# The up product of a feed-forward block, from feature-major to token-major in eleven tiles

## The chip, the cores and the metric

The kernel runs on one core of one Trainium2 chip. The metric is the device time of one execution in microseconds, as the median of several runs. Everything is float32 outside; inside, each operand of a large product is split into two fp32r parts (hi and lo), and a product is three matmuls: hi x hi, lo x hi, hi x lo.

## The reference

One layer of an encoder for 256 tokens of width 2048: two attention mixers on one normalised input, merged by gates, an output projection, and a feed-forward block with norms before and behind it. The change concerns the feed-forward block and the seam ahead of it:

```python
mixed = (g_sb * y_sb + g_mla * y_mla) @ w_out[l]
h = h + rms_norm(mixed, norm_post_mix[l])

gu = rms_norm(h, norm_pre_ffn[l]) @ w_gate_up[l]     # 2048 x 11264
g, up = gu[..., :D_FF], gu[..., D_FF:]               # D_FF = 5632
h = h + rms_norm((jax.nn.silu(g) * up) @ w_down[l], norm_post_ffn[l])
```

`rms_norm(x, gain)` is x / sqrt(mean(x^2) + 1e-6) * gain.

## The kernel before

Weights come from HBM in units of 128 x 1024 float32 (512 KB), each a DMA on SyncE's queue into one of four `raw` buffers. `unit` (line 87) splits a unit: ScalarE copies it to fp32r (`hi`, line 100), VectorE subtracts (`lo`, line 101); there are four buffers of each. TensorE then streams.

There are two forms of product. `pair` (line 155) is feature-major: a 128 x 128 block of weights is the stationary operand, and the activations stream past it, once 512 columns wide (hi and lo parts of 256 tokens, line 171) against the hi weights and once 256 wide (hi part alone, line 173) against the lo weights. Its result has features on the partitions and tokens on the columns, and hi and lo sums lie side by side, so that `fold` (line 179) has to add them. `token` (line 185) is token-major: 128 tokens are the stationary operand, 512 columns of weights stream past, three times (lines 207 to 209). The up product (`gu`) is in 44 `pair`s of 128 gate and 128 up features, 16 k-tiles each; the output projection (`wout`) and the down product (`wd`) are in `token` form, four blocks of 512 columns each.

Accumulators are pairs of PSUM banks (`mm_pair`), two pairs in all. Four more banks (`at_bank`) serve transposes and small products. 52 slots of 2 KB per partition (`slot`) hold what lives longer.

The seam. The last block of `wout` ends its first 128 tokens four units ahead of the second 128. As a half ends, `after_mix` sums its squares (ScalarE, line 658), takes the root (`neg_rsqrt`), scales and adds (`residual`, VectorE, line 701). The sums go through a multiplication with `norm_pre_ffn` (`gffn`, GpSimd, line 703; for the first quarter of the second half, in `first_parts`, as a scale on the copy instead), then through TensorE transposes (`turned`, line 710, or `first_residual`, line 723) into `hs`, the feature-major input of `gu`, again as hi and lo (lines 713 and 714, 730 and 732). The factor `r2` of the second norm comes later: it is worked out while the first `pair`s run, spread over the partitions by two small matmuls (line 761), and multiplied in `fold`. `hidden` then applies SiLU, multiplies gate and up, and splits the result, quarter tile by quarter tile of the hidden features, into `hid`, which is the stationary operand of `wd` as it stands.

The order on each engine is set by a scheduler from the order in which the code is written and its own estimates; `at_unit(n, f)` hangs a piece of work behind the n-th unit, and `tc.issue_after` keeps a group from being put ahead of a given instruction.

Of the kernel before, what the change touches and what calls it, by code (L numbers as in the profile page):

```python
# [52 lines left out]
def block_kernel(ctx: ExitStack, tc: tile.TileContext, a: dict, out: bass.AP):  # L53
# [101 lines left out]
    def pair(name, stream, K, per, rhs, first=None, eng=None, middle=None, after=None):  # L155
        ps = mm_pair(f"{name}_ps")
        for u in range(K // per):
            cuts = (4 if u == 0 else 2) if first else 1
            with ExitStack() as order:
                if after and u >= after[0]:  # L160
                    for ins in after[1:]:
                        order.enter_context(tc.issue_after(ins))
                hi, lo = unit(stream, per * 2 * P, cuts, eng(u) if eng else None, first and (lambda c: first(u, c)))
# [451 lines left out]

    gffn = []
    for n in range(4):
        g_t = slot(f"gffn{n}")
        G.dma_start(g_t.rearrange("p a b -> p (a b)"),
# [280 lines left out]
```

## Time and profile before

| | us |
|---|---|
| median of 3 runs (1410.33, 1410.45, 1412.1) | 1410.45 |
| profiled execution, first to last instruction | 1409.0 |
| TensorE busy in it | 1383.6 |
| up product, first to last matmul start | 660.7 to 1160.0 |
| down product | 1160.1 to 1399.5 |

The profile is of one execution. Times in its rows are microseconds from the span's start. A matmul's duration overlaps with the next one's, so what a step costs is the distance from one start to the next. The profile's "idle before" of an engine tells what it waited for; only waits on the chain that ends last cost time. The granted clock of TensorE has two levels, 1.0 (2.4 GHz) and 0.5 (1.2 GHz), and a mean over a stretch lies in between.

### The profile page before, as it was taken

To read this page: it belongs to the slowest core of one execution; us is meant where nothing else is said; L and a number is where in the kernel's file an instruction comes from. 1 tells how busy PE (TensorE), PEld (TensorE's weight loads), DVE (VectorE), ACT (ScalarE), POOL (GpSimd) and SP (SyncE) were. 2 spreads that over 40 slices of the span, in tenths; PEclk is the share of its full clock that TensorE was granted. 3 is DMA by queue.
4 is the path that set the end of the run, shared out by engine and by line. 5 is a ranking of instruction groups with operands and counts; after the bars stand their busy time and mean duration, and the time that the engine had idled before them with its cause. 6 is when DMAs were issued, how large, how long until landed. Compare 5 with 4: busy or idle time off the path is not lost.

```text
span 1409.0 us, 19102 instructions
## 1 busy us (share of the span) xinstructions
PE 1383.6 (98%) x7372; PEld 1186.8 (84%) x7372; DVE 883.6 (63%) x1109; ACT 710.7 (50%) x959; POOL 71.6 (5%) x93
## 2 busy tenths in 40 slices
PE   7999999999999999997999999999999999999997
PEld 6888888888888888886888888888888888888886
DVE  7996965555555687548666666666656565444444
ACT  7554454466658555445544444444444454434343
POOL 3210000000002200003000000000000001000000
PEclk9999999999999999999999999999999999999999
DMA  7565655455556765653655565556555556666653
GB/s 240 183 209 164 195 164 161 154 171 173 165 181 234 244 193 186 194 190 105 207 182 188 185 188 186 186 187 185 189 182 192 182 191 222 191 195 192 192 193 117
DMA packets 74668, 262.00 MB, mean 186 GB/s; under 512 B 8528, under 2 KB 9680, under 8 KB 74448
## 3 DMA queue, kind: packets, MB, share of 16 engines
q1 hardware_dynamic: 72720, 254.87, 56.7%
q0 software_dynamic: 1424, 5.24, 1.1%
q8 instruction: 58, 0.95, 0.3%
q10 hardware_dynamic: 432, 0.66, 0.1%
q14 instruction: 34, 0.28, 0.1%
HBM read 258.64 MB, written 2.10 MB: 185 GB/s over the span
## 4 chain that ended last, share of the span: by engine, by line
PE 93%; DVE 4%; ACT 1%; issue 1%; DMA 0%; SPq 0%; POOL 0%; DVEq 0%; ACTq 0%
PE gu_ps L171 23%; PE gu_ps L173 12%; PE gate_ps L171 8%; PE wd_ps L207 6%; PE wd_ps L208 6%; PE wd_ps L209 6%; PE gate_ps L173 4%; PE wo_ps L637 4%; PE q_sb_ps L171 2%; PE k_sb_ps L171 2%; PE wo_ps L638 2%; PE wout_ps L207 2%; PE wout_ps L208 2%; PE wout_ps L209 2%; PE q_sb_ps L173 1%; PE k_sb_ps L173 1%
## 5 line engine op out<-in xcount | busy, mean ns | idle before, releaser
L171 PE MATMUL gu_ps<-hs,hi_w_gu 128*128 128x512 f32 x1408 | 498.1, 399 | 0.2 <-DVE hs L732 0.2
L173 PE MATMUL gu_ps<-hs,lo_w_gu 128*128 128x256 f32 x1408 | 396.0, 281 | 0.0
L171 PEld LDWEIGHTS gu_ps<-hs,hi_w_gu 128*128 128x128 f32 x1408 | 264.8, 188 | 65.6 <-DVE hs L732 0.5
L101 DVE TENSOR_TENSOR lo_w_gu<-raw_w_gu,hi_w_gu 128x1024 fp32r<-128x1024 f32 x175 | 216.0, 1235 | 159.8 <-ACT hi_w_gu L100 159.7
L100 ACT ACTIVATE hi_w_gu<-raw_w_gu 128x1024 fp32r<-128x1024 f32 x176 | 185.7, 1056 | 195.0 <-issue 116.9
L173 PEld LDWEIGHTS gu_ps<-hs,lo_w_gu 128*128 128x128 f32 x1408 | 266.6, 189 | 0.1
L101 DVE TENSOR_TENSOR lo_w_down<-raw_w_down,hi_w_down 128x1024 fp32r<-128x1024 f32 x88 | 110.9, 1262 | 119.1 <-ACT hi_w_down L100 118.9
L171 PE MATMUL gate_ps<-xs,hi_w_gate 128*128 128x512 f32 x512 | 180.7, 398 | 0.0
L100 ACT ACTIVATE hi_w_down<-raw_w_down 128x1024 fp32r<-128x1024 f32 x88 | 93.3, 1061 | 135.5 <-PE wd_ps L208 125.1
L173 PE MATMUL gate_ps<-xs,lo_w_gate 128*128 128x256 f32 x512 | 143.2, 280 | 0.0
L207 PE MATMUL wd_ps<-hi_w_down,hid 128*128 128x512 f32 x352 | 137.2, 390 | 0.0
L208 PE MATMUL wd_ps<-hi_w_down,hid 128*128 128x512 f32 x352 | 137.1, 390 | 0.0
L209 PE MATMUL wd_ps<-lo_w_down,hid 128*128 128x512 f32 x352 | 137.1, 389 | 0.0
L101 DVE TENSOR_TENSOR lo_w_gate<-raw_w_gate,hi_w_gate 128x1024 fp32r<-128x1024 f32 x64 | 78.4, 1230 | 68.5 <-ACT hi_w_gate L100 68.5
L171 PEld LDWEIGHTS gate_ps<-xs,hi_w_gate 128*128 128x128 f32 x512 | 96.3, 188 | 22.5
L100 ACT ACTIVATE hi_w_gate<-raw_w_gate 128x1024 fp32r<-128x1024 f32 x64 | 67.5, 1056 | 58.2 <-PE gate_ps L171 46.5
L173 PEld LDWEIGHTS gate_ps<-xs,lo_w_gate 128*128 128x128 f32 x512 | 96.6, 189 | 0.0
L207 PEld LDWEIGHTS wd_ps<-hi_w_down,hid 128*128 128x128 f32 x352 | 66.1, 188 | 14.1 <-DVE r L665 0.3
L209 PEld LDWEIGHTS wd_ps<-lo_w_down,hid 128*128 128x128 f32 x352 | 66.1, 188 | 13.7
L208 PEld LDWEIGHTS wd_ps<-hi_w_down,hid 128*128 128x128 f32 x352 | 66.1, 188 | 13.5
L101 DVE TENSOR_TENSOR lo_w_out<-raw_w_out,hi_w_out 128x1024 fp32r<-128x1024 f32 x32 | 39.2, 1225 | 37.0 <-ACT hi_w_out L100 36.8
L100 ACT ACTIVATE hi_w_out<-raw_w_out 128x1024 fp32r<-128x1024 f32 x32 | 33.9, 1061 | 43.9 <-PE wout_ps L208 34.7
(346 smaller groups left out, 2197.5 us busy)
## 6 DMA issues: line engine op xcount, KB each, us to landing
raw_w_gu<-in_w_gu SPq DMA_DIRECT2D x176, 512.0 KB, 3.5
raw_w_down<-in_w_down SPq DMA_DIRECT2D x88, 512.0 KB, 4.3
raw_w_gate<-in_w_gate SPq DMA_DIRECT2D x64, 512.0 KB, 3.6
raw_w_o<-in_w_o SPq DMA_DIRECT2D x32, 512.0 KB, 3.6
raw_w_out<-in_w_out SPq DMA_DIRECT2D x32, 512.0 KB, 3.5
raw_w_lat<-in_w_lat SPq DMA_DIRECT2D x16, 512.0 KB, 4.7
raw_w_q<-in_w_q SPq DMA_DIRECT2D x16, 512.0 KB, 4.1
raw_w_k<-in_w_k SPq DMA_DIRECT2D x16, 512.0 KB, 3.5
```

The costliest lines, as they stand in the source:

```text
L100: split_ins[0] = S.activation(hi[:, cs], raw[:, cs], AF.Copy)
L101: mi = (eng or V).tensor_tensor(lo[:, cs], raw[:, cs], hi[:, cs].bitcast(F32), op=ALU.subtract)
L171: TE.matmul(ps[:, j, :], lhsT=hi[:, o:o + P], rhs=r, start=k == 0, stop=False, skip_group_check=True)
L173: mm = TE.matmul(ps[:, j, 0:T], lhsT=lo[:, o:o + P], rhs=r[:, 0], start=False, stop=k == K - 1, skip_group_check=True)
L207: TE.matmul(ps[t], lhsT=l[:, 0, ts], rhs=hi[:, cs], start=k == 0, stop=False)
L208: TE.matmul(ps[t], lhsT=l[:, 1, ts], rhs=hi[:, cs], start=False, stop=False)
L209: mm = TE.matmul(ps[t], lhsT=l[:, 0, ts], rhs=lo[:, cs], start=False, stop=k == K - 1)
L637: TE.matmul(ps[:, j, :], lhsT=hi[:, o:o + P], rhs=r, start=k == 0, stop=False, skip_group_check=True)
L638: mm = TE.matmul(ps[:, j, 0:T], lhsT=lo[:, o:o + P], rhs=r[:, 0], start=False, stop=k == 7, skip_group_check=True)
```

## The change

The up product becomes token-major. It is done in 11 tiles (`up`) of 512 gate and 512 up columns; a unit is one k-tile of both (`up_unit`). For each k-tile and each half of the tokens there are six matmuls of 512 columns: three into the gate bank and three into the up bank. Each half has a pair of banks, so a tile holds all four. Within a tile the halves are offset: the first half does `head` k-tiles alone at the start (six in the first tile, two in the others), and ends two k-tiles ahead of the second. `up_out` takes a half out of its banks: SiLU with the factor r2 as a scale per partition on ScalarE, and one VectorE product. The result has tokens on the partitions, so `up_turn` transposes it on TensorE, four 128 x 128 blocks to a group, two groups a tile, hung behind units of the next tile, and splits it into hi and lo for `wd`.

`norm_pre_ffn` moves into the weight split: `up_unit` scales with the gain of the k-tile's rows, on ScalarE in the copy and on VectorE as a three-operand instruction. The four loads of `gffn` and GpSimd's eight products go, as do `fold`, `hidden` and the small matmuls of `r2` for this product. The four k-tiles that come first are split in halves into slots, not buffers. Both halves of the tokens now go through `residual` and `turned` alike, and `first_residual`, `first_parts` and `later_residual` go; the first transposes are hung one unit earlier (6 for `TURN` = 7). The weights are laid out accordingly; their bytes and their units are the same.

```diff
-def pair(name, stream, K, per, rhs, first=None, eng=None, middle=None, after=None):
+def pair(name, stream, K, per, rhs, first=None):
...
-        r1s[t] = neg_rsqrt(ss1, t, "r1", None if t else lambda: mg_part(ps, t, 3))
-        if t == 0:
+        r1s[t] = neg_rsqrt(ss1, t, "r1", lambda: mg_part(ps, t, 3))
+        with tc.issue_after(ready[0][1]):
             for n in range(4):
-                residual(0, n)
-        else:
-            tp = first_residual()
-            with tc.issue_after(ready[0][1]):
-                first_parts(tp)
-                mg_part(ps, 1, 3)
-                for n in range(1, 4):
-                    turned(0, n)
+                residual(t, n)
...
         V.scalar_tensor_tensor(x_t, mg[t, n], r1s[t], x_t, op0=ALU.mult, op1=ALU.add)
-        hg = tmp.tile([P, 512], F32, tag="t2", name="hg", bufs=6)
-        G.tensor_tensor(hg, x_t, flat(gffn[n]), op=ALU.mult)
-        hgs[t, n] = hg
...
-            TE.transpose(tp[:, kk * P:kk * P + P], hgs[t, n][:, kk * P:kk * P + P], ident)
+            TE.transpose(tp[:, kk * P:kk * P + P], hres[t, n][:, kk * P:kk * P + P], ident)
...
-    at_unit(count[0] + TURN, lambda: turned(0, 0))
+    at_unit(count[0] + 6, lambda: turned(0, 0))
...
-    for f in range(KF):
-        waiting.append((f, pair(f"gu{f}", "w_gu", KD, 4, lambda k: hs[:, k], eng=(lambda u: G if u in GP else None) if f == 0 else None,
...
-        if f > 0:
-            while waiting:
-                hidden(*waiting.pop(0))
+    def up_unit(c, k):
...
+        nc.sync.dma_start(raw, src)
+        g = gf[:, k:k + 1]
+        if c == 0 and k < AHEAD:
+            hi, lo = [[flat(slot(f"{nm}_w_gu_{off}_{j}", F32R)) for j in range(2)] for nm in ("hi", "lo")]
+            for j in range(2):
+                cs = slice(j * 512, j * 512 + 512)
+                split_ins[0] = S.activation(hi[j], raw[:, cs], AF.Copy, scale=g)
+                split_ins[1] = V.scalar_tensor_tensor(lo[j], raw[:, cs], g, hi[j].bitcast(F32), op0=ALU.mult,
+                                                      op1=ALU.subtract)
+            return hi, lo
...
+        split_ins[0] = S.activation(hi, raw, AF.Copy, scale=g)
+        split_ins[1] = V.scalar_tensor_tensor(lo, raw, g, hi.bitcast(F32), op0=ALU.mult, op1=ALU.subtract)
...
+    def up_out(ps, t, hts):
...
+        S.activation(s, ps[:, 0], AF.Silu, scale=r2s[t])
...
+        V.scalar_tensor_tensor(ht, ps[:, 1], r2s[t], s, op0=ALU.mult, op1=ALU.mult)
+        hts.append(ht)
+
+    def up_turn(c, hts, i):
+        tp = at_bank(f"ht{c}{i}")
+        for j in range(2):
+            f = 2 * i + j
+            for t in range(2):
+                o = j * T + t * P
+                TE.transpose(tp[:, o:o + P], hts[t][:, f * P:f * P + P], ident)
...
+        S.activation(hi, tp, AF.Copy)
+        V.tensor_tensor(lo, tp, hi.bitcast(F32), op=ALU.subtract)
...
+    def up(c):
+        head, tail = (HEAD0 if c == 0 else HEAD), TAIL
+        order = [(k, t) for t in range(2) for k in range(head)]
+        order += [(k, t) for k in range(head, KD - tail) for t in range(2)]
+        order += [(k, t) for t in range(2) for k in range(KD - tail, KD)]
...
+            if c == 0 and (t, k) in turns:
+                for n in turns[t, k]:
+                    turned(t, n)
...
+            for j in range(2):
+                TE.matmul(ps[t][:, j], lhsT=hs[:, k, 0, ts], rhs=hi[j], start=k == 0, stop=False)
+                TE.matmul(ps[t][:, j], lhsT=hs[:, k, 1, ts], rhs=hi[j], start=False, stop=False)
+                mm = TE.matmul(ps[t][:, j], lhsT=hs[:, k, 0, ts], rhs=lo[j], start=False, stop=k == KD - 1)
...
+            if k == KD - 1:
+                up_out(ps[t], t, hts)
+        for i in range(2):
+            at_unit(count[0] + 1 + i, lambda i=i: up_turn(c, hts, i))
...
+    turns = {(0, 0): (1,), (0, 2): (2,), (0, 4): (3,), (1, 0): (0, 1), (1, 3): (2,), (1, 6): (3,)}
...
+    for c in range(KF // 4):
+        up(c)
```

Where the scheduler puts these things follows at two places. First TensorE's row at the seam. In it `tp` are the transposes; `hg` and `x_4364` are residuals (`x_4356` to `x_4362` the first half's quarters, `x_4364` to `x_4370` the second's). Before, the last transposes ahead of the first up matmul:

```order
L710 MATMUL tp_5963<-ident,hg 128x128
L723 MATMUL tp_5944<-ident,x_4364 128x128
L710 MATMUL tp_5970<-ident,hg 128x128 x4
L710 MATMUL tp_5977<-ident,hg 128x128 x4
L171 MATMUL gu_ps<-hs,hi_w_gu_5987 128x512
L173 MATMUL gu_ps<-hs,lo_w_gu_5988 128x256
```

Now, where `gu_ps_5934` is the first half's accumulator, `gu_ps_6044` the second's, and `hi_w_gu_0`, `hi_w_gu_1` are the gate and up halves of the first k-tile:

```order
L685 MATMUL tp_6019<-ident,x_4362 128x128 x4
L774 MATMUL gu_ps_5934<-hi_w_gu_0_5937,hs 128x512
L775 MATMUL gu_ps_5934<-hi_w_gu_0_5937,hs 128x512
L776 MATMUL gu_ps_5934<-lo_w_gu_0_5939,hs 128x512
L774 MATMUL gu_ps_5934<-hi_w_gu_1_5938,hs 128x512
L775 MATMUL gu_ps_5934<-hi_w_gu_1_5938,hs 128x512
L685 MATMUL tp_6045<-ident,x_4364 128x128 x4
L685 MATMUL tp_6052<-ident,x_4366 128x128 x4
L774 MATMUL gu_ps_6044<-hi_w_gu_0_5937,hs 128x512
L685 MATMUL tp_6077<-ident,x_4368 128x128 x4
L776 MATMUL gu_ps_5934<-lo_w_gu_1_5940,hs 128x512
```

The second half's first transposes (of `x_4364`) stood ahead of every up matmul, and stand behind five of them now.

Second, VectorE's row at the end of an up tile. Before, between two `pair`s:

```order
L101 TENSOR_TENSOR lo_w_gu_6427<-raw_w_gu_6425,hi_w_gu_6426 128x1024
L181 TENSOR_TENSOR s<-gu_ps,tb 128x512
L183 TENSOR_TENSOR s<-s,r_5984 128x512
L101 TENSOR_TENSOR lo_w_gu_6460<-raw_w_gu_6458,hi_w_gu_6459 128x1024
L773 TENSOR_TENSOR s<-s 128x256
L776 TENSOR_TENSOR hid_6355<-s,hid_6355 128x256
```

Now, at the end of the second tile (`gu_ps_6339` and `gu_ps_6364` are its two halves, `lo_w_gu_6659` is the first k-tile of the third tile):

```order
L731 SCALAR_TENSOR_TENSOR lo_w_gu_6659<-raw_w_gu_6656,packed,hi_w_gu_6658 128x1024
L731 SCALAR_TENSOR_TENSOR lo_w_gu_6671<-raw_w_gu_6668,packed,hi_w_gu_6670 128x1024
L738 SCALAR_TENSOR_TENSOR ht<-gu_ps_6339,r2p_6179,s 128x512
L731 SCALAR_TENSOR_TENSOR lo_w_gu_6705<-raw_w_gu_6702,packed,hi_w_gu_6704 128x1024
L731 SCALAR_TENSOR_TENSOR lo_w_gu_6732<-raw_w_gu_6729,packed,hi_w_gu_6731 128x1024
L738 SCALAR_TENSOR_TENSOR ht<-gu_ps_6364,r2p_6210,s 128x512
L731 SCALAR_TENSOR_TENSOR lo_w_gu_6750<-raw_w_gu_6747,packed,hi_w_gu_6749 128x1024
```

The four VectorE instructions of every quarter tile have become one product a half; that of the second half stands behind the splits of the next tile's third and fourth k-tile.

## Rows read from the trace of the kernel before

**Rows 1.** Page, parts 1 and 4: TensorE's totals; the chain's shares by engine.
```profile
PE 1383.6 (98%) x7372; PEld 1186.8 (84%) x7372; DVE 883.6 (63%) x1109; ACT 710.7 (50%) x959; POOL 71.6 (5%) x93
...
PE 93%; DVE 4%; ACT 1%; issue 1%; DMA 0%; SPq 0%; POOL 0%; DVEq 0%; ACTq 0%
```

**Rows 2.** Stretches: us, PE, PEld, DVE, ACT, POOL busy (count), clock, DMA share, GB/s.
```profile
700.00:800.00 100.00, 100.00 (x568) 86.77 (x567) 60.87 (x71) 47.55 (x63) 0.00 (x0) 1.00 0.59 187
...
1160.00:1399.00 239.00, 239.00 (x1055) 197.74 (x1054) 116.39 (x107) 99.05 (x106) 6.73 (x3) 1.00 0.59 185
```

**Rows 3.** Timeline of TensorE in the up product: start, us, line, operation, operands, count.
```profile
700.05 0.40 PE L171 MATMUL gu_ps<-hs,hi_w_gu 128*128 128x512 f32 x1
700.29 0.28 PE L173 MATMUL gu_ps<-hs,lo_w_gu 128*128 128x256 f32 x1
...
703.94 0.40 PE L171 MATMUL gu_ps<-hs,hi_w_gu 128*128 128x512 f32 x1
```

**Rows 4.** Views of tiles gu_ps, wd_ps: count, ns min/median/max, first and last start.
```profile
L171 PE MATMUL gu_ps<-hs,hi_w_gu x1408: 387/398/505, 660.7 to 1159.7; 128*128 128x512 f32 x176
...
L207 PE MATMUL wd_ps<-hi_w_down,hid x352: 388/390/505, 1160.1 to 1399.1; 128*128 128x512 f32 x176
```

**Rows 5.** Timeline of TensorE at the seam ahead of the up product.
```profile
649.17 0.40 PE L209 MATMUL wout_ps<-lo_w_out,mixed 128*128 128x512 f32 x1
...
657.16 0.48 PE L723 MATMUL tp<-ident,x 128*128 128x128 f32 x1 [7.16 <-DVE x L722]
...
660.75 0.51 PE L171 MATMUL gu_ps<-hs,hi_w_gu 128*128 128x512 f32 x1 [0.22 <-DVE hs L732]
```

**Rows 6.** Timeline of TensorE: a group of transposes inside the up product.
```profile
662.15 0.28 PE L173 MATMUL gu_ps<-hs,lo_w_gu 128*128 128x256 f32 x1
662.27 0.60 PE L710 MATMUL tp<-ident,hg 128*128 128x128 f32 x4
662.62 0.48 PE L171 MATMUL gu_ps<-hs,hi_w_gu 128*128 128x512 f32 x1
662.94 0.28 PE L173 MATMUL gu_ps<-hs,lo_w_gu 128*128 128x256 f32 x1
```

**Rows 7.** Durations: two lines' views (min/median/max ns), then groups (busy us, mean ns).
```profile
L710 PE MATMUL tp<-ident,hg x28: 270/273/422, 649.4 to 669.1; 128*128 128x128 f32 x28
...
L701 DVE SCALAR_TENSOR_TENSOR x<-mg,r,x x7: 739/748/1776, 646.2 to 665.3; 128x512 f32<-128x512 f32 x7
...
L101 DVE TENSOR_TENSOR lo_w_gu<-raw_w_gu,hi_w_gu 128x1024 fp32r<-128x1024 f32 x175 | 216.0, 1235 | 159.8 <-ACT hi_w_gu L100 159.7
...
L714 DVE TENSOR_TENSOR hs<-tp,hs 128x512 fp32r<-128x512 f32 x7 | 4.6, 682 | 0.3 <-ACT hs L713 0.3
...
L100 ACT ACTIVATE hi_w_gu<-raw_w_gu 128x1024 fp32r<-128x1024 f32 x176 | 185.7, 1056 | 195.0 <-issue 116.9 <-PE gu_ps L171 78.1
...
L116 ACT ACTIVATE xs<-xT,packed 128x256 fp32r<-128x256 f32 x16 | 7.5, 503 | 4.4 <-DMA xT<-in_xT 4.2
...
L100 ACT ACTIVATE hi_w_lat<-raw_w_lat 128x256 fp32r<-128x256 f32 x4 | 1.6, 408 | 0.7 <-DMA raw_w_lat<-in_w_lat 0.7
```

**Rows 8.** Timeline of ScalarE at the seam: the squares of either half.
```profile
644.16 0.60 ACT L658 ACTIVATE sqo<-wout_ps 128x512 f32<-128x512 f32 x1 [4.56 <-PE wout_ps L209]
...
649.60 0.60 ACT L658 ACTIVATE sqo<-wout_ps 128x512 f32<-128x512 f32 x1 [3.21 <-PE wout_ps L209]
```

**Rows 9.** Timeline of VectorE at the seam: the first half's residuals and a split.
```profile
646.24 4.79 DVE L701 SCALAR_TENSOR_TENSOR x<-mg,r,x 128x512 f32<-128x512 f32 x4
650.95 2.28 DVE L101 TENSOR_TENSOR lo_w_gu<-raw_w_gu,hi_w_gu 128x1024 fp32r<-128x1024 f32 x1
```

**Rows 10.** Timeline of GpSimd at the seam.
```profile
647.13 7.22 POOL L703 TENSOR_TENSOR hg<-x,gffn 128x512 f32<-128x512 f32 x4 [179.50 <-DVE x L701]
```

**Rows 11.** Stretches at the seam, columns as in rows 2: the granted clock.
```profile
654.00:655.00 1.00, 0.00 (x0) 0.00 (x0) 0.89 (x4) 1.00 (x2) 0.74 (x2) 0.50 0.65 147
...
660.00:661.00 1.00, 0.78 (x5) 0.54 (x5) 0.66 (x3) 1.00 (x4) 1.00 (x2) 0.96 0.04 16
```

More of the change, by code (lines that the diff above doesn't have):

```diff
@@ L85, in block_kernel, with unit @@
     streams, split_ins = {}, [None, None]
-    def unit(stream, cols_n, cuts=1, eng=None, first=None):
+    def unit(stream, cols_n, cuts=1, first=None):
         off = streams.get(stream, 0)
@@ L158, in pair @@
             cuts = (4 if u == 0 else 2) if first else 1
[L159 to L163, printed above, removed]
+            hi, lo = unit(stream, per * 2 * P, cuts, first and (lambda c: first(u, c)))
             for i in range(per):
                 k = u * per + i
-                if middle and i == per // 2:
-                    middle(u)
                 for j in range(2):
@@ L398, in proj_v @@
     def proj_v(c):
-        ps = token(f"v_sb{c}", "w_v", KD, xk)
+        ps = token(f"v_sb{c}", "w_v", KD, lambda k: halves(xk(k)))
         for t in range(2):
@@ L458, in block_kernel @@
     for c in range(2):
-        ps = token(f"vm{c}", "w_ukv", 4, lambda k: lat["kv", k])
+        ps = token(f"vm{c}", "w_ukv", 4, lambda k: halves(lat["kv", k]))
         for t in range(2):
@@ L614, in block_kernel @@
         gpost.append(g_t)
[L616 to L619, printed above, removed]
-                    a["norm_pre_ffn"][n * 512:(n + 1) * 512].partition_broadcast(P))
-        gffn.append(g_t)
     mixed = []
@@ L745, in block_kernel @@
             mg_part(ps[t], t, n)
-    at_unit(count[0] + TURN, lambda: turned(0, 0))
-    token("wout3", "w_out", KD, lambda k: mixed[k], after_mix)
-    r2 = const.tile([P, T], F32, tag="r", name="r2")
+    at_unit(count[0] + 6, lambda: turned(0, 0))
+    token("wout3", "w_out", KD, lambda k: halves(mixed[k]), after_mix)
+    r2s = [None, None]
     def ffn_squares(t):
@@ L766, in block_kernel @@
-    at_unit(count[0] + 6, ffn_scale)
-    hid = []
-    def hidden(f, ps):
-        s = tmp.tile([P, 2, T], F32, tag="t2", name="s", bufs=6)
-        fold(ps, r2, s)
-        S.activation(s[:, 0], s[:, 0], AF.Silu)
-        V.tensor_tensor(s[:, 0], s[:, 0], s[:, 1], op=ALU.mult)
-        t = slot(f"hid{f}", F32R)
-        S.activation(t[:, 0], s[:, 0], AF.Copy)
-        V.tensor_tensor(t[:, 1], s[:, 0], t[:, 0].bitcast(F32), op=ALU.subtract)
-        hid.append(t)
-    r1_ready = ready[0]
-    waiting = []
@@ L781, in block_kernel, with ffn_scale @@
-    for f in range(KF):
-        waiting.append((f, pair(f"gu{f}", "w_gu", KD, 4, lambda k: hs[:, k], eng=(lambda u: G if u in GP else None) if f == 0 else None,
-                                middle=later_residual if f == 0 else None,
-                                after=(HOLD, *r1_ready) if f == 0 else None)))
-        if f > 0:
-            while waiting:
-                hidden(*waiting.pop(0))
+    def ffn_scale(t):
+        r2s[t] = const.tile([P, 1], F32, tag=f"r2p{t}", name=f"r2p{t}")
+        V.tensor_scalar_mul(r2s[t], neg_rsqrt(ss2, t, "r2"), -1.0)
```

82 lines of the change are left out of this document (37 added, 45 removed).

## The prediction

> **What bounds the kernel now.** I read the page's totals and its chain first. TensorE is busy for 98% of the span and carries 93% of the chain that ended last [rows 1], so an edit elsewhere pays only where TensorE waits for it. The table of stretches comes next: in the up product TensorE is busy for all of 700 to 800 us and in the down product for all of 1160 to 1399, at a granted clock of 1.00 (the 2.4 GHz level), with GpSimd idle in the first [rows 2]. A full stretch is shortened only by a cheaper stream, so I looked for the price of one step of each form.
>
> In the up product of before, eleven pairs (512 columns, then 256) go from 700.05 to 703.94: 353.6 ns a pair [rows 3]. In the down product, which has the token-major form already, each third matmul is of the first line; 352 of these start from 1160.1 to 1399.1, so 1053 steps take 239.0 us: 227.0 ns for 512 columns [rows 4]. A pair's 768 columns are one and a half such steps, 340.5 ns. The last look is at the seam ahead of the up product: the last matmul of the output projection starts at 649.17, its successor's place would be 649.40, and the first up matmul starts at 660.75 [rows 5]: 11.35 us, with 20 of the 32 transposes of the block's own input in it and a wait of 7.16.
>
> **The up stream.** Before: 1408 pairs x 353.6 = 497.9 us, and four groups of transposes or small matmuls inside it at 0.44 (below) make 499.7; the rows give 660.7 to 1160.1 or 499.4 [rows 4], so there is no hidden stall in it. After: 11 tiles x 16 k x 2 halves x 2 banks x 3 = 2112 matmuls of 512 columns, x 227.0 = 479.4 us. That is 18.5 us less. What carries it is that the same columns come in 2112 instructions instead of 2816. The Trainium skill ("TensorE: Matmul & The Clock Gate", Back-to-back issue gap) gives N/2.4 + 2.5 ns for one matmul at 2.4 GHz; by that a pair would take 325.0 ns and a 512 step 215.8, and the change would save 1.8 us here. The trace does not agree (353.6 and 227.0), and the measured steps are used.
>
> **The transposes of the output.** 11 tiles x 2 groups of 4. A group inside the stream of before: the 256-column matmul starts at 662.15, the transposes at 662.27, the next 512 at 662.62 and its partner at 662.94 [rows 6]. Without the group 662.15 to 662.94 would be one pair, 0.354, so it costs 0.44 us (0.11 each). 22 x 0.44 = 9.7 us, all on TensorE: 20 groups (8.8) in the up product, 2 (0.9) in the down product. The upper end is the whole duration of a transpose, 0.273 [rows 7], x 88 = 24.0 us, 14.3 more; I take 0.44, since that row is the same operation in the same stream. The Trainium skill (same page, Part 4: PE-mode transpose) gives some 275 ns for one in a kernel's context; our rows show that duration, but four in 0.44 us of stream. By its figure as a cost the sum would be 14.3 us worse, which is rival 2.
>
> Up stage: 479.4 + 8.8 = 488.2 against 499.4, **-11.2**; down stage **+0.9**.
>
> **The seam.** The first half of the tokens goes as before: squares at 644.16 [rows 8], first residual at 646.24 [rows 9]. There the four residuals take 4.79 us and the weight split behind them 2.28, twice their usual 0.75 and 1.23 [rows 7, 9], beside GpSimd's four gain products [rows 10]. These go with the gain's move into the weights, so the four end at about 649.0 instead of 651.0. One group of transposes now stands ahead of the last six matmuls of the projection, so these end at 649.84; three groups follow.
> The second half's squares start 0.44 later than 649.60 [rows 8], at 650.04. The first half needed 2.08 us from there to its first residual (644.16 to 646.24). VectorE's queue now has two subtracts (0.68) and a half weight split (0.75, the three-operand form) in between; less 0.08 of overlap each that is 1.87. So the residual starts at 653.9 and its four pieces end at about 656.6. The order of the change has the transposes of this half on TensorE behind only five up matmuls, so the offset of the halves, written as six k, is worth little at the start. Behind them TensorE is fed by VectorE: half split (0.67), subtract (0.60), half split (0.75), to 658.6. Until then TensorE has had 7 groups (3.1) and 9 matmuls (2.0) of the 8.7 us since 649.84: 3.6 idle. From there the splits run ahead: at 12 matmuls (2.72 us) a k-tile against 1.30 for a split. So the seam costs 3.6 + 8 groups x 0.44 = 7.1 instead of 11.35: -4.2. The clock: before, after TensorE's wait of 7 us, the granted clock stood at 0.50 (1.2 GHz) from 654 on and was back at 0.96 in 660 to 661 [rows 11]. The gaps are now below 1 us each, and no row shows whether such a stretch keeps the clock. If it falls and comes back some 2 us into the dense stream, that costs 1 us; I take 1, with ends 0 and 3. **-3.2**.
>
> **What is hidden.** The gain rides on the splits. ScalarE with a scale per partition takes 503 ns for 256 columns against 408, so 95 more: 1.15 for a split of 1024 (1.06 without). VectorE's three-operand form takes 748 for 512 against 682, 66 more: 1.30 for a split [rows 7]. Per k-tile of 2.72 us both have room, and a tile of 43.6 us loads VectorE with 16 x 1.30 + 2 x 0.75 + 2 x 0.68 = 23.7. The fold, the r2 product and SiLU on quarter tiles go, which bounds nothing. The weights come at 512 KB per 2.72 us; the down product moves them so already, at 185 GB/s without a stall [rows 2]. The four gain loads that go were covered. All this costs 0.
> The one tight place is the tile's end, since both halves hold all four accumulator banks. Put E at the start of a tile's last matmul. Bank 2 is wanted 15 steps later, at E + 3.40. To free it, VectorE's product stands behind two weight splits in the order, and the second waits for a buffer which the tile's last k-tile holds. A waiter starts 0.43 behind a matmul's start (649.17 to 649.60, [rows 5, 8]): the last reader of that buffer lies one step ahead, so E + 0.20, then 1.15 + 1.30 + 0.75 - 0.08 = E + 3.3. It fits by 0.1, and I put the nine such seams at 0, with an upper end of 0.7 each (6 us) if the splits are 0.3 longer.
>
> **Sum.** The profiled execution spans 1409.0; the median is 1410.45, 1.45 more, which I keep. 1409.0 - 11.2 + 0.9 - 3.2 = 1395.5, so **1396.9 us**, 1.0% faster. By itself this case reaches from 1392.3 (no idle and no lost clock at the seam) to 1400.
>
> **Rivals.**
> 1. The offset does nothing: the order puts the second half's transposes so early that the seam is as long as before, 11.35, with up to 2 us at the low clock: 1401 to 1403. For it: five matmuls only stand ahead of that wait. Against it: VectorE's residuals lose GpSimd's company. 10%.
> 2. Each transpose costs its duration: +14.3, 1411.2, no change. Against it: the group in the stream. 3%.
> 3. The tile's end stalls a little, 0.3 to 0.7 at nine seams: 1400 to 1403. For it: 0.1 us of slack. 8%.
> 4. **Slower**: the same place, with the 1024-column split in its three-operand form at the 2.28 that one split of before took [rows 9]. Then the two splits in series end at about E + 4.5, the product at E + 5.2; nine stalls of 1.8 make 16, and some 2 at the seam: 1415. It decides from a split of 2.2 us on. Against it: GpSimd is idle in the up product [rows 2], and the form costs 66 ns more at 512 columns. 2%.
> 5. **Slower**: the token-major step costs the pair's price per column, 353.6 x 512 / 768 = 235.7 instead of 227.0, so that only the transposes are left: +18.4, 1415. That is where the skill's formula above would lead too (16.7 less saved). Against it: 1053 steps at 227.0. 2%.
>
> **Chances.** Forecast 72%, rivals 10, 3, 8, 2 and 2; 3% for something else, a third on each side and in the middle. The range is 1392 to 1404: it leaves out rivals 2, 4 and 5 and some of the rest. About 0.2% (2.8 us) is what a measurement of this kernel can tell from no change. Faster 91%, same 4%, slower 5%.
>
> **What would show it.** Up stream: 512-column steps of 227 ns; 226 would be 2 us less, 236 rival 5. A transpose group from matmul to matmul: 0.44 more than a step. Seam: from the last projection matmul to a dense stream; TensorE waits of about 3.6 us in all for VectorE and ScalarE, the granted clock beside them. Tile ends: no TensorE wait for the product that reads the second bank. First down matmul about 15 us earlier than 1160.1. The prediction is wrong if TensorE waits inside the tiles, for weights or for banks, by over 0.3 us a tile.

## The result, and the profile after

The changed kernel takes 1397.2 us (median; 1397.0 to 1397.4), the kernel before on the same chip 1411.3 (1410.3 to 1412.4): a ratio of 0.990, interval 0.989 to 0.992. The profiled execution spans 1395.3 us against 1409.0. The forecast was 1396.9, with a span of 1395.5. Of 48 further runs of the kernel before, timed beside the experiments below, 43 took 1409.9 to 1412.5 us and five 1401.5 to 1402.8, against which the change gains only 5 us, while the runs of no other kernel here lie more than 3.4 us apart.

The page of the changed kernel: busy time by engine, the chain that ended last, and two of its costliest groups (busy us, mean ns of one, idle time before and its releaser). They answer to [rows 1, 3, 7].

```profile
PE 1376.4 (99%) x6752; PEld 1156.1 (83%) x6752; DVE 825.4 (59%) x975; ACT 702.5 (50%) x872; POOL 56.1 (4%) x81
...
PE 94%; DVE 3%; issue 1%; ACT 1%; DMA 0%; SPq 0%; POOL 0%; DVEq 0%; ACTq 0%
...
L731 DVE SCALAR_TENSOR_TENSOR lo_w_gu<-raw_w_gu,packed,hi_w_gu 128x1024 fp32r<-128x1024 f32 x172 | 220.9, 1284 | 212.8 <-ACT hi_w_gu L730 211.3
L730 ACT ACTIVATE hi_w_gu<-raw_w_gu,packed 128x1024 fp32r<-128x1024 f32 x172 | 197.9, 1152 | 229.3 <-PE gu_ps L775 225.6
```

TensorE still sets the time. The splits with the gain take 1.28 and 1.15 us (forecast: 1.30 and 1.15).

TensorE's timeline inside a tile (start, duration, engine, line): two rows 24 steps apart; the table of stretches for 700 to 800 us [rows 2]; and from the tile rows (first and last start) the down product [rows 4].

```profile
741.65 0.39 PE L775 MATMUL gu_ps<-hi_w_gu,hs 128*128 128x512 f32 x1
...
747.09 0.39 PE L775 MATMUL gu_ps<-hi_w_gu,hs 128*128 128x512 f32 x1
...
700.00:800.00 100.00, 100.00 (x453) 82.42 (x452) 53.50 (x48) 47.33 (x47) 0.00 (x0) 1.00 0.61 187
...
L200 PE MATMUL wd_ps<-hi_w_down,hidh x352: 388/389/497, 1145.6 to 1385.4; 128*128 128x512 f32 x176
```

A step takes 5.44 / 24 = 226.7 ns. The seam's timeline on TensorE, then VectorE's residuals of the first half (the second half's, at 653.12, took 2.73), then one stretch of it (busy us of PE, PEld, DVE, ACT, POOL, then the granted clock); before, these were [rows 5, 9, 11].

```profile
649.35 1.47 PE L685 MATMUL tp<-ident,x 128*128 128x128 f32 x12
651.48 0.50 PE L774 MATMUL gu_ps<-hi_w_gu,hs 128*128 128x512 f32 x1 [0.65 <-ACT hi_w_gu L724]
...
652.59 0.50 PE L776 MATMUL gu_ps<-lo_w_gu,hs 128*128 128x512 f32 x1 [0.37 <-DVE lo_w_gu L725]
...
657.83 0.50 PE L776 MATMUL gu_ps<-lo_w_gu,hs 128*128 128x512 f32 x1
...
645.73 2.74 DVE L679 SCALAR_TENSOR_TENSOR x<-mg,r,x 128x512 f32<-128x512 f32 x4
...
652.00:654.00 2.00, 1.42 (x4) 0.51 (x4) 2.00 (x5) 1.01 (x2) 0.00 (x0) 1.00 0.00 0
```

Instead of one wait of 7.16 us there are waits of at most 0.65, and the granted clock stays at 1.00 in this execution. From 649.35 to 657.83, where the stream becomes dense, are 8.48 us; 7 groups of transposes (3.1) and 9 matmuls (2.0) leave 3.4 idle.

Where the time went: from the projection's end to the first down matmul it was 649.40 to 1160.1, 510.7 us. It is now 648.91 to 1145.6, 496.7 (649.35 less the group that moved ahead of the last six matmuls): -14.0. The down product takes 239.8 instead of 239.0: +0.8. The part ahead of the seam was 0.5 shorter in this execution. Sum -13.7.

### The profile page after: what moved, and what is told of

The parts are those of the page before. It is cut to its first block, busy times and chain, and to the rows that moved or that the text cites. A ratio compares the mean times of both kernels' runs of the same rounds, so it can differ in the third digit from the quotient of the medians.

```text
span 1395.3 us, 17558 instructions
## 1 busy us (share of the span) xinstructions
PE 1376.4 (99%) x6752; PEld 1156.1 (83%) x6752; DVE 825.4 (59%) x975; ACT 702.5 (50%) x872; POOL 56.1 (4%) x81
## 4 chain that ended last, share of the span: by engine, by line
PE 94%; DVE 3%; issue 1%; ACT 1%; DMA 0%; SPq 0%; POOL 0%; DVEq 0%; ACTq 0%
PE gu_ps L774 12%; PE gu_ps L776 11%; PE gu_ps L775 11%; PE gate_ps L164 9%; PE wd_ps L200 6%; PE wd_ps L201 6%; PE wd_ps L202 6%; PE gate_ps L166 4%; PE wo_ps L624 4%; PE k_sb_ps L164 2%; PE q_sb_ps L164 2%; PE wo_ps L625 2%; PE wout_ps L200 2%; PE wout_ps L201 2%; PE wout_ps L202 2%; PE k_sb_ps L166 1%
## 5 line engine op out<-in xcount | busy, mean ns | idle before, releaser
L731 DVE SCALAR_TENSOR_TENSOR lo_w_gu<-raw_w_gu,packed,hi_w_gu 128x1024 fp32r<-128x1024 f32 x172 | 220.9, 1284 | 212.8 <-ACT hi_w_gu L730 211.3
L730 ACT ACTIVATE hi_w_gu<-raw_w_gu,packed 128x1024 fp32r<-128x1024 f32 x172 | 197.9, 1152 | 229.3 <-PE gu_ps L775 225.6
L774 PE MATMUL gu_ps<-hi_w_gu,hs 128*128 128x512 f32 x704 | 276.5, 393 | 0.7 <-ACT hi_w_gu L724 0.7
L776 PE MATMUL gu_ps<-lo_w_gu,hs 128*128 128x512 f32 x704 | 275.1, 391 | 0.7 <-DVE lo_w_gu L725 0.7
L775 PE MATMUL gu_ps<-hi_w_gu,hs 128*128 128x512 f32 x704 | 273.4, 389 | 0.0
L774 PEld LDWEIGHTS gu_ps<-hi_w_gu,hs 128*128 128x128 f32 x704 | 132.2, 188 | 30.2 <-DVE ht L738 2.2
L776 PEld LDWEIGHTS gu_ps<-lo_w_gu,hs 128*128 128x128 f32 x704 | 132.2, 188 | 28.9 <-DVE lo_w_gu L725 1.4
L775 PEld LDWEIGHTS gu_ps<-hi_w_gu,hs 128*128 128x128 f32 x704 | 132.2, 188 | 26.8
L200 PE MATMUL wd_ps<-hi_w_down,hidh 128*128 128x512 f32 x352 | 137.2, 390 | 0.0
L202 PE MATMUL wd_ps<-lo_w_down,hidh 128*128 128x512 f32 x352 | 137.0, 389 | 0.0
L201 PE MATMUL wd_ps<-hi_w_down,hidl 128*128 128x512 f32 x352 | 137.0, 389 | 0.0
L200 PEld LDWEIGHTS wd_ps<-hi_w_down,hidh 128*128 128x128 f32 x352 | 66.1, 188 | 14.1 <-DVE r L652 0.3
```

The source lines that it names most:

```text
L200: TE.matmul(ps[t], lhsT=l[0][:, ts], rhs=hi[:, cs], start=k == 0, stop=False)
L201: TE.matmul(ps[t], lhsT=l[1][:, ts], rhs=hi[:, cs], start=False, stop=False)
L202: mm = TE.matmul(ps[t], lhsT=l[0][:, ts], rhs=lo[:, cs], start=False, stop=k == K - 1)
L730: split_ins[0] = S.activation(hi, raw, AF.Copy, scale=g)
L731: split_ins[1] = V.scalar_tensor_tensor(lo, raw, g, hi.bitcast(F32), op0=ALU.mult, op1=ALU.subtract)
L774: TE.matmul(ps[t][:, j], lhsT=hs[:, k, 0, ts], rhs=hi[j], start=k == 0, stop=False)
```

## Experiments

All times are medians, and the differences are against the change's 1397.2. The kernels were timed in three groups, each beside runs of the kernel before, whose median was 1410.7 to 1411.2 there. The change itself was not timed again beside them, so a difference of about 1 us counts only where a trace shows it at its place.

**1 and 2. The price of the output's transposes.** In the first kernel the loop over the four transposes of `up_turn` stands twice; in the second it is left out.

```diff
 def up_turn(c, hts, i):
...
-        for j in range(2):
-            f = 2 * i + j
-            for t in range(2):
-                o = j * T + t * P
-                TE.transpose(tp[:, o:o + P], hts[t][:, f * P:f * P + P], ident)
...
-        S.activation(hi, tp, AF.Copy)
-        V.tensor_tensor(lo, tp, hi.bitcast(F32), op=ALU.subtract)
+        S.activation(hi, hts[0].rearrange("p (j t) -> p j t", j=2), AF.Copy)
+        V.tensor_tensor(lo, hts[1].rearrange("p (j t) -> p j t", j=2), hi.bitcast(F32), op=ALU.subtract)
```

> Each of the 22 groups of four transposes of the up product's output is issued twice, so 88 more transposes stand in TensorE's stream; nothing else changes. Theory of the prediction (a group in the stream costs 0.44 us): 22 x 0.44 = +9.7 us, 1406.9. Rival 2 (each transpose costs the 0.273 us that its row shows): +24.0, 1421.2. A third reading, that the groups lie in time that TensorE waits anyway: +0, 1397.2.

> The 88 transposes of the up product's output are left out: ScalarE and VectorE split the token-major product itself instead of its transpose, so the down product multiplies the wrong layout, with the same number of instructions. Theory: 22 x 0.44 = -9.7 us, 1387.5. Rival 2: -24.0, 1373.2. If the groups were covered by waits: 0, 1397.2.

Measured: doubled 1407.0 (1406.4 to 1408.1), +9.8, which is 0.45 us for a group; left out 1386.6 (1386.2 to 1387.5), -10.6, 0.48 a group. Rival 2 (+24, -24) falls. TensorE's timeline of the doubled kernel, at one group:

```profile
751.01 0.40 PE L781 MATMUL gu_ps<-lo_w_gu,hs 128*128 128x512 f32 x1
751.25 0.60 PE L747 MATMUL ht<-ident,ht 128*128 128x128 f32 x4
751.68 0.60 PE L752 MATMUL ht<-ident,ht 128*128 128x128 f32 x4
752.04 0.47 PE L781 MATMUL gu_ps<-lo_w_gu,hs 128*128 128x512 f32 x1
```

The second four begin 0.43 behind the first: 0.11 each, though one shows 0.27 as its duration. In the traces a tile lasts 45.47 us doubled, 44.60 in the change and 43.63 without the transposes, so 0.43 and 0.48 a group, as the medians say. The doubled kernel's trace shows one more thing, at the seam, where its code is that of the change: the waits are the same (0.65, 0.37, 0.21), but the granted clock fell behind them.

```profile
651.28 0.50 PE L779 MATMUL gu_ps<-hi_w_gu,hs 128*128 128x512 f32 x1 [0.65 <-ACT hi_w_gu L724]
...
654.00:655.00 1.00, 1.00 (x6) 0.98 (x6) 1.00 (x3) 0.14 (x1) 0.00 (x0) 0.50 0.00 0
```

It was back at 1.00 before 658, and the up stream ran about 0.5 us later than in the change.

**3. What a step costs apart from its columns.**

```diff
-                TE.matmul(ps[t][:, j], lhsT=hs[:, k, 0, ts], rhs=hi[j], start=k == 0, stop=False)
-                TE.matmul(ps[t][:, j], lhsT=hs[:, k, 1, ts], rhs=hi[j], start=False, stop=False)
-                mm = TE.matmul(ps[t][:, j], lhsT=hs[:, k, 0, ts], rhs=lo[j], start=False, stop=k == KD - 1)
+                for a, b, st, sp in ((0, hi, k == 0, False), (1, hi, False, False), (0, lo, False, k == KD - 1)):
+                    for q in ([slice(0, 512)] if st or sp else [slice(0, 256), slice(256, 512)]):
+                        mm = TE.matmul(ps[t][:, j, q], lhsT=hs[:, k, a, ts], rhs=b[j][:, q], start=st, stop=sp,
+                                       skip_group_check=True)
```

> All up matmuls but the first and the last of each accumulation (k 1 to 14, and parts of k 0 and 15) are issued as two of 256 columns: the same columns in about 2000 more instructions (2112 steps, of which 44 first and 44 last ones stay whole: 2024 more). Theory (what the change saves is the price per instruction): a pair of before took 353.6 ns and a 512 step 227.0, so a 256 step takes 126.6, two of them 253.2, 26.2 ns more than a whole one; x 2024 = +53 us, about 1450. Rival 5's reading (a price per column): 0, 1397.2. The Trainium skill (TensorE: Matmul & The Clock Gate, Back-to-back issue gap) has 2.5 ns for each further instruction: +5 us, 1402.

Measured: 1425.6 (1423.8 to 1426.6), +28.4: 14.0 ns for each of the 2024 further instructions. Rival 5's price per column falls, but so does my figure of 26.2. TensorE's timeline in a tile (x is how many in a row):

```profile
720.38 0.64 PE L776 MATMUL gu_ps<-hi_w_gu,hs 128*128 128x256 f32 x4
...
723.98 0.28 PE L776 MATMUL gu_ps<-hi_w_gu,hs 128*128 128x256 f32 x1
```

30 steps in 3.60 us, 120.0 ns each. With 226.7 for 512 columns, 256 columns cost 106.7 and the instruction (a matmul with its weight load) 13.3. The Trainium skill ("TensorE: Matmul & The Clock Gate", Back-to-back issue gap) has N/2.4 + 2.5 ns: the slope agrees (256 / 2.4 = 106.7), the constant doesn't (13.3). A pair of before should then take 226.7 + 120.0 = 346.7. It took 353.6 [rows 3], so 6.9 were without a reason.

**4 and 5. What else the pair cost.** In the first kernel the change's matmuls are given the widths of before (512, 256, 512, 256); in the second the kernel before is given two of 512, then two of 256.

```diff
+                steps = [(0, hi, 0, 512), (1, hi, 0, 512 if last else 256), (0, lo, 0, 512)]
+                if not last:
+                    steps.append((1, hi, 256, 512))
...
-                for j in range(2):
+                for j, part in ((0, 0), (1, 0), (0, 1), (1, 1)) if stream == "w_gu" else ((0, 0), (0, 1), (1, 0), (1, 1)):
```

> In every k but the last of each accumulation the middle one of three up matmuls (512 columns, hi weights by the low part of the tokens) is cut into two of 256, and one of them is put behind each of the other two: 512, 256, 512, 256, the order of widths that the kernel before has, with the same columns as the change and 11 x 15 x 4 = 660 more instructions. The run with 256-column halves gave 120.0 ns for a step of 256 among its like, and the change has 226.7 for 512. Theory A (a price per instruction and nothing else): 660 x (2 x 120.0 - 226.7 = 13.3) = +8.8 us, 1406. Theory B (a narrow matmul beside a wide one costs more than among its like, as the pair of before did: 353.6 against 226.7 + 120.0 = 346.7): 660 x 2 x 6.9 = 9.1 us more, +17.9, 1415.

> The kernel before, with one edit: in its up product the two 512-column matmuls of a k-tile stand together, then its two of 256, instead of 512, 256, 512, 256. Same instructions, half as many changes of width. Theory B of the run above (the change of width costs 6.9 ns a pair): 704 x 6.9 = -4.9 us, 1406.3. Theory A (no such cost, the 6.9 belongs to something else in the pair): 0, 1411.2.

Measured: mixed 1413.2 (1411.5 to 1414.9), +16.0 (16.2 in the traces, from the first to the last up matmul); grouped 1404.6 (1403.7 to 1405.3), 6.4 less than before, ratio 0.996 (0.995 to 0.997). Theory A (+8.8 and 0) misses twice. TensorE's timeline, of the mixed kernel and of the grouped one:

```profile
719.76 0.40 PE L779 MATMUL gu_ps<-lo_w_gu,hs 128*128 128x512 f32 x1
720.00 0.63 PE L779 MATMUL gu_ps<-hi_w_gu,hs 128*128 128x256 f32 x3
...
723.30 0.40 PE L779 MATMUL gu_ps<-lo_w_gu,hs 128*128 128x512 f32 x1
```

```profile
699.68 0.63 PE L172 MATMUL gu_ps<-hs,hi_w_gu 128*128 128x512 f32 x2
700.15 0.39 PE L175 MATMUL gu_ps<-hs,lo_w_gu 128*128 128x256 f32 x2
...
703.86 0.40 PE L172 MATMUL gu_ps<-hs,hi_w_gu 128*128 128x512 f32 x1
```

Mixed: ten pairs (the x3 are 256, 512, 256) in 3.54 us, 354.0 ns each, the pair of before to half a nanosecond, in another layout and with other weights. Grouped: twelve pairs in 4.18, 348.3; the edit also lets the two banks take turns. So the order of the widths matters here, but theory B's fixed price for a change of width does not hold either: with half as many changes 5.3 of the 6.9 ns are gone, and the kernel before has pairs without them. Two stretches of its gate product follow, which lies ahead of the changed part, from the same line and with the same turns of 512 and 256:

```profile
428.04 0.40 PE L171 MATMUL gate_ps<-xs,hi_w_gate 128*128 128x512 f32 x1
...
432.28 0.40 PE L171 MATMUL gate_ps<-xs,hi_w_gate 128*128 128x512 f32 x1
...
455.30 0.39 PE L171 MATMUL gate_ps<-xs,hi_w_gate 128*128 128x512 f32 x1
...
459.46 0.39 PE L171 MATMUL gate_ps<-xs,hi_w_gate 128*128 128x512 f32 x1
```

Twelve pairs take 4.24 us in the first stretch, 353.3 ns each (the 353.6 of [rows 3] are eleven pairs of such a stream), and 4.16 in the second, 346.7, which is 226.7 + 120.0 with nothing left over; the granted clock is 1.00 in both. From 278 us to the end of the up product, each stretch of 14 or more pairs that nothing breaks has one of these two paces. The gate product goes from one to the other at its breaks (small matmuls of other work), all is at 346.7 from 451 to 561 us, and the up product is at 353.3 from 683 to 1160, where nothing breaks it. In the mixed kernel one tile of eleven took the lower pace (45.5 us for it, 46.1 for most others).

So of the 353.6 - 1.5 x 226.7 = 13.6 ns that the change saves per pair, half an instruction is 6.6, and the rest is the slower pace at which the pairs of before ran. What picks the pace stays open. At the lower one the up product of before would take 1408 x 6.6 ns = 9.3 us less, an estimate. The five shorter runs of the kernel before are shorter by 9; no trace of them is kept, so it is not shown that this is the reason.

**6, 7 and 8. The tile's end.** HEAD and TAIL are the k-tiles by which one token half runs ahead at a tile's ends; they become 0 in the first kernel (diff) and 3 in the second; the third kernel splits the weights without the gain.

```diff
-HEAD = 2
-TAIL = 2
+HEAD = 0
+TAIL = 0
```

```diff
-        split_ins[0] = S.activation(hi, raw, AF.Copy, scale=g)
-        split_ins[1] = V.scalar_tensor_tensor(lo, raw, g, hi.bitcast(F32), op0=ALU.mult, op1=ALU.subtract)
+        split_ins[0] = S.activation(hi, raw, AF.Copy)
+        split_ins[1] = V.tensor_tensor(lo, raw, hi.bitcast(F32), op=ALU.subtract)
```

> HEAD and TAIL from 2 to 0: the two token halves of a tile run in step from its first k to its last, with no offset at the ten inner tile ends (the first tile's head keeps its 6). Theory: with E the start of a half's last matmul, its second bank comes free at E + 3.3 us, by the trace of the change (E 743.9, next use 747.3). It is then wanted 9 steps later, at E + 2.0, so each tile end waits 1.3 us for the first half and up to as much again for the second: +13 to +26 us, 1410 to 1423. Rival: VectorE and ScalarE free the banks sooner when they are asked to, and the offset is worth nothing: 0 to +2, 1397 to 1399.

> HEAD and TAIL from 2 to 3: at each of the ten inner tile ends the halves are offset by three k-tiles instead of two, so a bank is wanted 21 steps (4.8 us) after the start E of a half's last matmul, not 15 (3.4). Theory: a tile takes 44.60 us where 192 steps of 226.7 ns and two groups of 0.44 make 44.40; the 0.2 comes from the second bank, free at E + 3.3 to 3.4, and from the slower steps behind that break. With 1.4 us more room it goes: -0.2 x 10 = -2, 1395.2, and the steps behind the tile's start are 226.7 instead of 231 to 233. Rival: the 0.2 belongs to the transposes and the fetch of other work: 0, 1397.2. Second rival: three k-tiles held for both halves leave one of four weight buffers free, so TensorE waits for splits, 0.3 to 0.5 a tile: +3 to +5, 1400 to 1402.

> The splits of all w_gu tiles but the first four of the first column tile are a plain copy and a plain subtract, as before the change: norm_pre_ffn is left out there. Theory: the gain costs ScalarE and VectorE time that TensorE's stream covers; only at the tile's end the two splits ahead of the product shorten by 0.07 + 0.08, which takes the 0.1 us wait at the second bank away: 0 to -2 us, 1395.2 to 1397.2. Rival: the splits set the pace of the stream (1.28 us of VectorE per k-tile beside its other work), and the steps get faster all along: -4 or more, 1393 or less.

Measured: offset 0 1406.8 (1405.8 to 1408.1), +9.6; offset 3 1396.3 (1395.7 to 1396.8), -0.9; plain split 1398.4 (1397.5 to 1398.8), +1.2. The change at the place, on VectorE and TensorE, with the table of waits for 690 to 1140 us (sum, times, longest):

```profile
743.94 2.65 DVE L731 SCALAR_TENSOR_TENSOR lo_w_gu<-raw_w_gu,packed,hi_w_gu 128x1024 fp32r<-128x1024 f32 x2 [0.84 <-ACT hi_w_gu L730]
746.50 0.75 DVE L738 SCALAR_TENSOR_TENSOR ht<-gu_ps,r2p,s 128x512 f32<-128x512 f32 x1
...
743.91 0.39 PE L776 MATMUL gu_ps<-lo_w_gu,hs 128*128 128x512 f32 x1
...
747.31 0.49 PE L774 MATMUL gu_ps<-hi_w_gu,hs 128*128 128x512 f32 x1
747.64 0.39 PE L775 MATMUL gu_ps<-hi_w_gu,hs 128*128 128x512 f32 x1
...
749.95 0.39 PE L776 MATMUL gu_ps<-lo_w_gu,hs 128*128 128x512 f32 x1
...
PEld gu_ps L774 <- DVE ht L738: 2.2, 9, 0.3
```

E is 743.91. The product that frees the bank ends at 747.25, E + 3.34 as forecast, and the matmul that wants it starts at 747.31, on time. But its weight load had waited, and the next matmul comes 0.33 later instead of 0.23; the ten behind it take 0.231 each (747.64 to 749.95). A tile lasts 44.60 us (first groups of transposes at 750.18 and 794.78), with offset 3 44.46: 0.14 at each of nine ends, 1.3 us, and its table of waits has no such line. The rest of the 0.2 is behind the groups. Three k-tiles held did no harm inside these tiles. In the first tile, though, TensorE waited 0.80 us for one split of ScalarE, which stood behind another that had waited 1.67 us for its weights; from the projection to the down product this trace is only 0.35 shorter than the change's.

Offset 0, the same place on TensorE and VectorE, and its last tile's end at the down product:

```profile
745.62 0.39 PE L776 MATMUL gu_ps<-lo_w_gu,hs 128*128 128x512 f32 x1
746.29 0.50 PE L774 MATMUL gu_ps<-hi_w_gu,hs 128*128 128x512 f32 x1 [0.28 <-DVE ht L738]
...
744.29 1.29 DVE L731 SCALAR_TENSOR_TENSOR lo_w_gu<-raw_w_gu,packed,hi_w_gu 128x1024 fp32r<-128x1024 f32 x1 [1.44 <-ACT hi_w_gu L730]
745.50 0.74 DVE L738 SCALAR_TENSOR_TENSOR ht<-gu_ps,r2p,s 128x512 f32<-128x512 f32 x1
...
1151.22 0.39 PE L776 MATMUL gu_ps<-lo_w_gu,hs 128*128 128x512 f32 x1
1153.89 0.50 PE L200 MATMUL wd_ps<-hi_w_down,hidh 128*128 128x512 f32 x1 [2.28 <-DVE ht L738]
1154.23 0.59 PE L201 MATMUL wd_ps<-hi_w_down,hidl 128*128 128x512 f32 x1
...
1155.04 0.63 PE L200 MATMUL wd_ps<-hi_w_down,hidh 128*128 128x512 f32 x1
...
1157.60 0.43 PE L200 MATMUL wd_ps<-hi_w_down,hidh 128*128 128x512 f32 x1
...
1155.00:1156.00 1.00, 1.00 (x4) 0.76 (x3) 0.91 (x2) 0.00 (x0) 0.00 (x0) 0.50 1.06 393
```

My 13 to 26 was too much, for a reason: with the halves in step only one split stands ahead of the product, not two, and it ends E + 2.0 instead of E + 3.3 (E is 744.26 here). A tile lasts 45.06, so the offset is worth 0.46 at nine of the ten inner ends; the first one waits longer, 1.1 us. The rest is the last end: the down product waits 2.28 us, and then eight steps take 3.37 us at a granted clock down to 0.50 (1.2 GHz) instead of 1.8.

The plain split's product comes 0.16 sooner after E, as the shorter splits say, and yet the sum of that wait is 2.9 instead of 2.2, and a tile lasts 44.69. The edit had also changed the order on TensorE: the matmul on the second bank now stands one step earlier (0.23). So leaving the gain out bought nothing, but this run doesn't measure the gain by itself.

**9. GpSimd beside VectorE.**

```diff
         V.scalar_tensor_tensor(x_t, mg[t, n], r1s[t], x_t, op0=ALU.mult, op1=ALU.add)
+        G.tensor_tensor(spare, x_t, flat(gpost[n]), op=ALU.mult)
```

> GpSimd multiplies each finished residual by another tile into a spare one that nothing reads, four products beside each half's residuals, as its gain products stood there before the change. Theory: VectorE's residuals take twice as long beside GpSimd, 4.8 us for four instead of 2.74, and the splits and subtracts behind them too while GpSimd's eight products run on (7.2 us for four): the second half's transposes come 2 us later at least, more with the splits: +3 to +8 at the seam, 1400 to 1405. Rival: the 4.79 of before was due to something else there, and GpSimd takes nothing from VectorE: 0, 1397.2.

Measured: 1404.0 (1402.9 to 1404.8), +6.8. VectorE's and GpSimd's timelines at the seam, and a stretch behind it:

```profile
646.88 4.79 DVE L681 SCALAR_TENSOR_TENSOR x<-mg,r,x 128x512 f32<-128x512 f32 x4
651.60 0.68 DVE L692 TENSOR_TENSOR hs<-tp,hs 128x512 fp32r<-128x512 f32 x1
...
660.12 1.75 DVE L728 SCALAR_TENSOR_TENSOR lo_w_gu<-raw_w_gu,packed,hi_w_gu 128x512 fp32r<-128x512 f32 x1
...
647.79 6.38 POOL L682 TENSOR_TENSOR spare<-x,gpost 128x512 f32<-128x512 f32 x4 [182.33 <-DVE x L681]
...
662.00:664.00 2.00, 2.00 (x7) 1.60 (x8) 2.00 (x3) 0.00 (x0) 1.01 (x1) 0.50 0.40 117
```

4.79 is [rows 9] again: the products on GpSimd had made the residuals 1.75 times as long (4.79 for 2.74), and the split behind them takes 1.75 instead of 0.74. TensorE waits 2.63 us for that split, and behind it the granted clock is 0.50. Putting GpSimd back beside both halves costs more than the seam had gained (4.1, below). The Trainium skill (GPSIMD Engine Reference, Key points) says that GpSimd contends with VectorE instructions that have two SBUF inputs. The trace agrees: residuals and splits have two and are slowed, while the subtract at 651.60, whose other input lies in PSUM, keeps its 0.68 beside a busy GpSimd.

**10, 11 and 12. The seam's order.** The first kernel has no offset in the first tile. The second issues the first three k-tiles' splits ahead of the squares (EARLY is 3), and queues the others behind the second half's square root and residuals (ready1). The third does that with offset 3.

```diff
-HEAD0 = 6
+HEAD0 = 0
```

```diff
     def after_mix(ps, t):
+        if t == 0:
+            for k in range(EARLY):
+                early[k] = up_unit(0, k)
         squares(ss1, ps, t, 3)
...
-                w[k] = up_unit(c, k)
+                if c == 0 and k in early:
+                    w[k] = early.pop(k)
+                elif c == 0:
+                    with tc.issue_after(ready1[0]), tc.issue_after(ready1[1]):
+                        w[k] = up_unit(c, k)
```

> HEAD0 from 6 to 0: in the first column tile the code writes the two token halves k by k, with no offset of six k-tiles; the second half's four groups of transposes then stand behind eight up matmuls instead of five, and spread wider. Theory: the offset at the seam is worth little, since VectorE's queue of residuals, subtracts and splits sets the idle time there: 0 to +1, 1397.2 to 1398.2. Rival: the offset of the halves is what shortens the seam, and without it the idle time goes back towards the 7 us of before: +3 to +4, 1400 to 1401.

> At the seam only: the splits of the first three k-tiles of w_gu are issued ahead of the squares and residuals of the block's input, where ScalarE is idle from 639.1 to 643.6 us and VectorE from 640.3 to 644.4, and the splits from the fourth k-tile on are queued behind the second half's residuals. Theory: the 3.4 us that TensorE is idle between the last projection matmul and the dense stream come from VectorE's queue, where half splits, subtracts and residuals alternate. With 18 matmuls of the first half ready, TensorE has work until the second half's transposes can start: idle 1 us, -2.4, 1394.8. Rival: the chain over squares, root and residuals sets the end, and the splits beside it are covered: 0, 1397.2. Second rival: the splits delay the first half's squares: +1 to +2.

> Both at once: the first three k-tiles' splits ahead of the residuals, and HEAD and TAIL 3. Theory: the two gains are in different places and add: -2.4 - 2 = -4.4, 1392.8. Rival: one of them is nothing: 1394.8 to 1395.2. If both rivals hold: 1397.2 or slower.

Measured: no offset 1398.1 (1397.6 to 1398.6), +0.9; early splits 1394.55 (1393.4 to 1395.4), -2.65; both 1392.7 (1392.6 to 1393.0), -4.5, ratio to before 0.988 (0.985 to 0.992). Without the offset TensorE's first wait at the seam is 1.53 us instead of 0.65, and the clock stays at 1.00 all the same. Both edits together meet the expected -4.4; the two gains measured singly add up to -3.55, since the 0.80 us in the first tile of offset 3 are missing here. The ratios' intervals touch that of the change, but the ranges of the runs lie below its 1397.0 to 1397.4. The timeline of the last kernel at the seam, VectorE and TensorE (the edit has shifted the line numbers):

```profile
642.23 2.74 DVE L683 SCALAR_TENSOR_TENSOR lo_w_gu<-raw_w_gu,packed,hi_w_gu 128x512 fp32r<-128x512 f32 x4 [0.46 <-ACT hi_w_gu L682]
...
649.45 0.60 PE L713 MATMUL tp<-ident,x 128*128 128x128 f32 x4
649.81 0.48 PE L786 MATMUL gu_ps<-hi_w_gu,hs 128*128 128x512 f32 x1
...
654.94 1.36 PE L713 MATMUL tp<-ident,x 128*128 128x128 f32 x11
```

TensorE goes from the projection's last matmul into the up product with hardly a gap: 20 matmuls of the first half stand between the transposes. This kernel is faster than the change and than the kernel before.

## Why the prediction was right, point by point

- **The up stream (-18.5).** The price was right: 226.7 ns a step for 227.0. The reason given, fewer instructions for the same columns, was half of it; the other half is that the pairs of before ran at the slower of their two paces (experiments 3 to 5). The forecast didn't need the split, since both prices were read whole from rows of the product itself, but it holds for an execution of the kernel before at that pace only. The expectation for experiment 3, which did need it, failed by 25 us.
- **The transposes (+9.7).** Right kind, slightly small: 0.45 to 0.48 a group, so about 10.4. Behind a group the steps run at 0.23 for a while (below), which the row of before could not show.
- **The seam (-3.2).** Residuals at 2.74 and idle time of 3.4 (3.6) as worked out. Of the -14.0 up to the down product, the up stage has -9.9 (-11.2 forecast, -0.6 for the step, +0.6 for groups, +1.3 for ends), so the seam has -4.1. Of the 1 us put in for the clock none was lost in the change's trace, nor in six other traces with the same seam; in the doubled kernel's, with the same waits of up to 0.65, about 0.5 was. Leaving the term uncertain, between 0 and 3, was right. Larger losses are in experiments 6 and 9: waits of 2.3 and 2.6 us, then 0.50. That the offset is worth little there held (+0.9).
- **Hidden work (0).** Held inside the tiles. In the first tile it is close: ScalarE's splits wait there for their weights, which cost TensorE 0.08 us in the change's trace and 0.80 in that of offset 3.
- **The tile's end (0).** The product came at E + 3.34 for E + 3.3, but the slack of 0.1 us (0.06 in the trace) was not enough for the weight load ahead of the matmul: 0.14 at nine ends, 1.3 us. I had asked only when the matmul may start. Rival 3 had 0.3 to 0.7.
- **Sum.** What came better: the clock that was not lost (-1), the faster step (2112 x 0.3 ns, -0.6), and -0.5 ahead of the seam. What came worse: tile ends (+1.3) and groups (+0.7). They nearly cancel, and the span came out 0.2 off. The mechanisms were right but for the reason of the up stream, half of which was the pace that the kernel before ran at; that the sum is so close is luck of about 1 us.

## What to carry to other kernels

Price a stream by the distance of equal starts in the stretch of just that pattern of widths, since one width's price doesn't give a mixture's, and look at more than one stretch, since the mixture had two prices in one trace; and price a small matmul by what it pushes back, not by its duration. When an accumulator bank changes hands, the weight load ahead of the first matmul needs the slack too, so leave more than 0.1 us. Work that is ready early (here splits of weights) belongs ahead of a chain of dependent small steps, and a GpSimd operation beside a VectorE chain on the critical path is not free.

## What the runs showed of the hardware

- A 512-column step after a 512 takes 226.7 ns, a 256 among 256s 120.0, and a 512 and a 256 in turn either 346.7 a pair, which is their sum, or 353.3. A stretch that nothing breaks keeps its pace; what picks it is open.
- At a granted clock of 0.50 a 512-column step took 427 ns (1155.04 to 1157.60 in experiment 6, six steps), not twice 226.7: that is twice the 213.3 of the columns alone (106.7 for 256), so the 13 ns of the instruction do not show there.
- Behind a break (a group of transposes, or a late weight load) steps take 0.231 to 0.233 us instead of 0.2267, for ten steps or so (747.64 to 749.95 above). With that a group costs 0.47, not 0.44: a tile of 44.46 us less 192 x 0.2267 leaves 0.94 for two. Why the steps are longer is open.
- Beside GpSimd (busy from 647.79 to 654.17 and again from 656.32), VectorE's operations with all inputs in SBUF took 1.75 times as long and more (residuals 4.79 for 2.74, a split 1.75 for 0.74), and those with an input in PSUM no longer.
- Behind a wait of 2.28 us TensorE's granted clock was at 0.50, and eight steps cost 1.6 us more. Waits of 0.65 and less, 3.4 us idle within 8.5, left it at 1.00 in seven traces and not in an eighth; one wait of 1.53 left it at 1.00. So in these runs the length of a wait does not tell by itself whether the clock falls.
